# Second layer's input projections moved behind the whole first layer, with turned keys held on chip

## The chip, the core and the metric

The kernel runs on one core of one Trainium2 chip. The core has five engines with a queue each: PE (TensorE, matrix multiplies and their weight loads), DVE (VectorE), ACT (ScalarE), POOL (GpSimd) and SP (SyncE, which here issues nearly all DMA transfers). An engine works through its queue in order; an instruction that waits for a semaphore holds up all that stand behind it. The metric is the device time of one execution in microseconds (us), the median of several runs.

## What is computed

A decoder trunk of two layers over 2048 tokens of width 1024, all in float32. Layer 1 is an mLSTM mixer, layer 2 a dilated sliding-window attention; each is followed by a gated side term (`ple_add`). Keys and values of layer 2 come from the residual stream behind layer 1. Cut to layer 2, which the change is about:

```python
def shared_kv(h, norm_g, w_kv, knorm_g, cos, sin):          # 4 heads of 128
    k, v = jnp.split(rms_norm(h, norm_g) @ w_kv, 2, axis=-1)
    return apply_rope(rms_norm(k, knorm_g), cos, sin), v

def dilated_layer(h, k, v, norm_g, w_in, qnorm_g, w_out, cos, sin):
    q, z = jnp.split(rms_norm(h, norm_g) @ w_in, [1536], axis=-1)
    q = apply_rope(rms_norm(q, qnorm_g), cos, sin)          # 3 groups of 4 heads
    for g, (window, dilation) in enumerate(((128, 1), (512, 4), (2048, 16))):
        # query t sees t, t-r, t-2r, ..., t-window (r = dilation)
        o_g, l_g = dilated_window_attention(q[:, :, g], k, v, window, dilation)
    o = sum over g of softmax(l)[g] * o_g                   # l: log denominators
    return (o * silu(z)) @ w_out

h = h + mlstm_layer(h); h = ple_add(h)                      # layer 1
h = h + dilated_layer(h, *shared_kv(h)); h = ple_add(h)     # layer 2
```

The attention works on blocks of 128 queries: tokens of one residue modulo the dilation, against the 128 keys of the same block and, from the second block on, the 128 keys of the block before. Dilation 1 has 16 blocks, dilation 4 has 4 residues with 4 blocks each, dilation 16 has 16 residues with one block each.

## The kernel before

**Tiles.** The tokens are worked on in `NG` = 4 groups of `T` = 512 (`NT` = 4 tiles of 128 tokens). Activations X are kept as 8 pieces of 128 features by 512 tokens, each split into a high and a low fp32r part (`xh`, `xl`; `split`, L99 to L107). Weights are streamed from memory for each group: a raw piece (`wraw`, `raw_piece`, 5 buffers), its two parts (`wh`, `wl`, 5 buffers each), then three matmuls for each of four outputs (high by high, low by high, high by low).

**Projections.** `project` (L153) runs over the 8 pieces; one piece, 12 matmuls of 512 columns, is called a *step*. With `feat` set the outputs are features by tokens (L167), otherwise tokens by features (L169). Behind each step it calls a hook, if there is one for that step, and `pump`, which advances the list `side` by one turn. In this way work of other kinds stands between the steps on every engine's queue.

**Order.** For each group: `a_in` (projections and mLSTM of layer 1), `a_out` (output projection and `ple`, which writes h to `h2d` and splits h into X for layer 2), then `b_in`: keys, values, queries of dilation 16 (`queries(2)`), of dilation 4 and of dilation 1, and the gate z, six projections of 8 steps. Keys and queries go through `normrope` (norm and rotation, on DVE, ACT and POOL) and, like the values, to memory: `kd`, `vd`, `qd`.

**Attention.** A block is the generator `attend`, with five stages: load keys and queries (`kr`, `qr`); turn them by four transposes each on PE (`turned`, L664) and copy the result to `kT` (ACT) and `qT` (DVE); scores (L695) and softmax (L701 to L707); transposes of the probabilities (L715); product with the values (L726). A block whose predecessor isn't at hand also loads and turns the keys of the block before (`kp`). `staged` starts a block each turn and moves all started ones by a stage. The first list (14 blocks of dilation 4 and 1) runs beside the last group's `b_in`; at `late`, behind `queries(2)`, a second list is added with the remaining two, all of dilation 16, the last blocks of dilation 4, the four combinations `held_back` and the blocks of group 1 of dilation 1.

**Combination and end.** Dilation 4 and 16 leave their results in memory (`o1d`, `o2d`, with maxima and sums in 8 more columns). `combine` loads both (`oo`, 2 buffers) and `zt` (1 buffer), forms the weights and the sum y (L760 to L778, DVE and ACT) and multiplies by z (L780, POOL). y is turned (`transposed`, L182) and goes into the output projection and the second `ple`, again by groups, with the remaining blocks of dilation 1 between the steps.

The order on each queue is made by a scheduler from the order of the code and priorities (`PRE` for weights, `EVAC` for what empties a bank); buffers of one name are handed out in turn, and a tile waits until the one that had its buffer is read.

## Time and profile before

| | us |
|---|---|
| median of three runs | 2348.1 (2347.1 to 2356.36) |
| the profiled execution, whole | 2347.66 |
| its span, first to last instruction | 2345.8 |
| its mean granted TensorE clock | 0.997 |

The table's last three rows are of the one execution that the profile shows. The chain of work in order of time and the timelines place the parts of the program in the span: layer 1 and the `b_in` of the first three groups, and the last group's layer 1 but for its end, up to 1544 us; the last group's output projection and `ple`; its `b_in` with attention beside it from 1646.7 to 1932.3 us; a stretch of attention blocks and combinations without projections up to 1962.1 us; then the output projections of layer 2 to the end. In the 40 slices of the page these are slices 28 to 34.

PE's rows print a duration that runs on into the next instruction, since matmuls are pipelined. The distance between the starts of neighbouring rows is what an instruction takes from the queue.

### The profile page before, as it was taken

The numbers are of one execution on the slowest core, as the hardware profiler recorded it, in microseconds if no ns is written. First come the engines' busy times: TensorE is split into PE (matmuls) and PEld (weight loads), VectorE is DVE, ScalarE is ACT, GpSimd is POOL, SyncE is SP. The second block draws the span as 40 slices with busy tenths as digits, with TensorE's granted clock in tenths as the row PEclk, the third lists the DMA queues.
The fourth block names the chain that finished last, engine by engine and source line by source line (L and its number), as shares of the span: only waits on it lengthen the run. The fifth ranks groups of instructions, "written<-read, shape, count | busy, mean of one in ns | idle before, by whom it ended". The sixth has DMA issues, their size and how long they took to land.

```text
span 2345.8 us, 35374 instructions
## 1 busy us (share of the span) xinstructions
PE 2313.6 (99%) x11760; PEld 1977.5 (84%) x11760; DVE 1543.6 (66%) x3405; ACT 1128.3 (48%) x2731; POOL 593.0 (25%) x719
## 2 busy tenths in 40 slices
PE   9999999999999999999999999999999998999999
PEld 7889888888888888889888888888898887888887
DVE  6846665776566667747575675566755668786866
ACT  5434454543344545434444543344664666453643
POOL 5011235601211644011225601212202121220301
PEclk9999999999999999999999999999999999999999
DMA  5433344533244455333344543253674777465453
GB/s 184 125 91 115 99 149 162 183 116 121 61 123 125 146 164 165 117 91 111 103 130 142 174 125 120 64 171 117 203 221 134 231 237 228 135 198 164 145 160 98
DMA packets 190246, 337.14 MB, mean 144 GB/s; under 512 B 21552, under 2 KB 38256, under 8 KB 190064
## 3 DMA queue, kind: packets, MB, share of 16 engines
q1 hardware_dynamic: 189920, 334.86, 46.1%
q8 instruction: 93, 1.52, 0.3%
q14 instruction: 89, 0.73, 0.1%
q10 hardware_dynamic: 144, 0.02, 0.0%
HBM read 284.27 MB, written 50.53 MB: 143 GB/s over the span
## 4 chain that ended last, share of the span: by engine, by line
PE 85%; DVE 6%; DMA 4%; POOL 2%; ACT 2%; issue 1%; SPq 0%; ACTq 0%; DVEq 0%; POOLq 0%
PE bank L169 41%; PE bank L167 32%; PE bank L726 2%; PE bank L695 2%; PE bank L664 1%; DVE wl L104 1%; PE bank L525 1%; PE bank L526 1%; PE bank L528 1%; PE bank L715 1%; PE bank L182 1%; DMA oo<-o2d 1%; PE bank L512 1%; DMA o2d<-ot 1%; DVE xl L106 1%
## 5 line engine op out<-in xcount | busy, mean ns | idle before, releaser
L169 PE MATMUL bank<-wh,xh 128*128 128x512 f32 (+1 forms) x1664 | 642.5, 386 | 2.8 <-ACT wh L102 2.8
L169 PE MATMUL bank<-wl,xh 128*128 128x512 f32 (+1 forms) x1664 | 622.0, 374 | 0.8 <-DVE wl L104 0.8
L169 PE MATMUL bank<-wh,xl 128*128 128x512 f32 (+1 forms) x1664 | 622.6, 374 | 0.0
L102 ACT ACTIVATE wh<-wraw 128x512 fp32r<-128x512 f32 (+1 forms) x544 | 326.7, 603 | 549.5 <-PE bank L167 302.8
L104 DVE TENSOR_TENSOR wl<-wraw,wh 128x512 fp32r<-128x512 f32 (+1 forms) x512 | 353.9, 695 | 318.7 <-ACT wh L102 317.3
L167 PE MATMUL bank<-xh,wh 128*128 128x512 f32 x1272 | 501.9, 395 | 0.4 <-ACT xh L102 0.4
L167 PE MATMUL bank<-xh,wl 128*128 128x512 f32 x1272 | 496.0, 390 | 0.0
L167 PE MATMUL bank<-xl,wh 128*128 128x512 f32 x1272 | 495.9, 390 | 0.0
L169 PEld LDWEIGHTS bank<-wh,xh 128*128 128x128 f32 x1664 | 313.9, 189 | 51.0 <-ACT wh L102 3.1
L169 PEld LDWEIGHTS bank<-wh,xl 128*128 128x128 f32 x1664 | 313.4, 188 | 50.3
L169 PEld LDWEIGHTS bank<-wl,xh 128*128 128x128 f32 x1664 | 314.2, 189 | 49.3 <-DVE wl L104 1.2
L206 POOL TENSOR_TENSOR acc<-acc,sq 128x512 f32<-128x512 f32 x105 | 162.1, 1545 | 546.7 <-ACT sq L205 543.8
L167 PEld LDWEIGHTS bank<-xl,wh 128*128 128x128 f32 x1272 | 239.1, 188 | 50.5
L167 PEld LDWEIGHTS bank<-xh,wh 128*128 128x128 f32 x1272 | 239.4, 188 | 48.3 <-ACT xh L102 0.6
L167 PEld LDWEIGHTS bank<-xh,wl 128*128 128x128 f32 x1272 | 239.6, 188 | 47.8
L106 DVE SCALAR_TENSOR_TENSOR wl<-wraw,gam,wh 128x512 fp32r<-128x512 f32 x192 | 159.8, 833 | 154.1 <-ACT wh L102 151.5
L102 ACT ACTIVATE wh<-wraw,gam 128x512 fp32r<-128x512 f32 x192 | 138.0, 721 | 195.2 <-PE bank L169 134.8
L707 ACT ACTIVATE pr<-pr,nm 128x256 f32<-128x256 f32 (+1 forms) x192 | 86.6, 453 | 43.5 <-DVE nm L704 43.3
L601 POOL TENSOR_SCALAR ssb<-ssb,r 128x4 f32<-128x4 f32 x64 | 27.3, 426 | 254.1 <-ACT jk L194 233.0
L695 PE MATMUL bank<-kT,qT 128*128 128x128 f32 x600 | 78.5, 278 | 7.0 <-DVE pT L719 2.9
L695 PEld LDWEIGHTS bank<-kT,qT 128*128 128x128 f32 x600 | 72.8, 192 | 10.5 <-DVE pT L719 4.5
L726 PEld LDWEIGHTS bank<-vt,pT 128*128 128x128 f32 x600 | 75.3, 194 | 3.9
(413 smaller groups left out, 2957.4 us busy)
## 6 DMA issues: line engine op xcount, KB each, us to landing
wraw<-in_w_pg SPq DMA_DIRECT2D x128, 256.0 KB, 2.8
wraw<-in_w_in_b SPq DMA_DIRECT2D x128, 256.0 KB, 2.8
wraw<-in_w_z SPq DMA_DIRECT2D x96, 172.0 KB, 2.3
wraw<-in_w_v SPq DMA_DIRECT2D x64, 256.0 KB, 2.6
wraw<-in_w_o SPq DMA_DIRECT2D x64, 256.0 KB, 2.7
wraw<-in_w_out_a SPq DMA_DIRECT2D x64, 256.0 KB, 2.6
wraw<-in_w_kv SPq DMA_DIRECT2D x64, 256.0 KB, 2.7
kr<-kd SPq DMA_DIRECT2D x53, 256.0 KB, 4.2
```

The source lines that it names most:

```text
L102: nc.scalar.mul(dst_h, src, scale)
L104: nc.vector.tensor_tensor(dst_l, src, dst_h.bitcast(F32), op=ALU.subtract)
L106: nc.vector.scalar_tensor_tensor(dst_l, src, scale, dst_h.bitcast(F32), op0=ALU.mult, op1=ALU.subtract)
L167: nc.tensor.matmul(acc[i], w[:, cs], x, start=first, stop=last)
L169: nc.tensor.matmul(acc[i][:, :n], x[:, cs], w, start=first, stop=last)
L182: nc.tensor.transpose(tp[:, t * P:(t + 1) * P], tiles[t][:, k * P:(k + 1) * P], ident)
L206: eng.tensor_tensor(acc, acc, sq, op=ALU.add)
L512: nc.tensor.matmul(sp[:, h * P:(h + 1) * P], qk[:, NH + h, ts_], qk[:, h, ts_], start=True, stop=True)
L601: nc.gpsimd.tensor_scalar(ss, ss, r2[:, t:t + 1], EPS, op0=ALU.mult, op1=ALU.add)
L695: nc.tensor.matmul(sp[:, hh * n + j * P:hh * n + (j + 1) * P], qT[:, hs], kvs[j]["k"][:, hs], start=True, stop=True)
L707: nc.scalar.activation(pr[:, hh, :n], pr[:, hh, :n], AF.Exp, bias=nm[:, h:h + 1], accum_out=md[:, 4 + h:5 + h])
L726: nc.tensor.matmul(op[:, hs], pTs[h // 2][:, c0 + j * P:c0 + (j + 1) * P], kvs[j]["v"][:, hs], start=j == 0, stop=j == nk - 1)
```

## The change

- The loop over the groups runs all of layer 1 first; `b_in` follows for all four groups, as a phase of its own. `a_out` no longer splits h into X; `b_in` loads X from `h2d` (8 pieces for each group). The token norms for `b_in` (`rstb`) are made by a hook behind step `BH` = 3 of the following projection.
- `b_in` begins with `queries(2)`, then keys, values, the queries of dilation 4 and 1, and z.
- Keys aren't written to memory. `turn_key` transposes each tile of 128 tokens once, by hooks behind steps 3 to 6 of the value projection, into `kT`, which holds all keys (128 by 4 heads by 2048 tokens). `attend` reads the keys of a block out of `kT` with a step of 1, 4 or 16 columns.
- Attention blocks begin as soon as their group's projections are done: 8 blocks beside `b_in(1)`, 4 beside `b_in(2)`, 4 beside `b_in(3)`, the rest from two steps (`VP`) behind the values of the last group.
- Buffers: `wraw` 5 to 4, `pj` 8 to 7, `oo` 2 to 1; `kr` (2) and the 4 small `kT` are gone; `xraw` lives in another pool.

```diff
-        raw = wp.tile([P, n], F32, name="wraw", tag="wraw", bufs=5)
+        raw = wp.tile([P, n], F32, name="wraw", tag="wraw", bufs=4)
...
-        return sm.tile([P, n], F32, name="pj", tag="pj", bufs=8)
+        return sm.tile([P, n], F32, name="pj", tag="pj", bufs=7)
...
         def done(k, hk):
-            X2.append(new_x())
-            split(*X2[k], hk, 1.0)
             squares(sq2, k, hk)
             nc.sync.dma_start(h2d[g, k], hk)
 
         ple(0, g, h, X, sq, done)
-        return X2, sq2
+        return {BH: lambda: rstb.append(token_rstd(sq2, "rstb"))}
...
-    def b_in(g, X, sq, late=lambda: None):
+    def b_in(g, late=lambda: None, hooks={}):
+        X = []
+        for k in range(KD):
+            with tc.high_priority(offset=PRE):
+                raw = raw_piece(h2d[g, k], T)
+                X.append(new_x())
+                split(*X[k], raw, 1.0)
...
+        def keys():
+            acc = project(I["w_kv"][0], 512, 8, X, False, gam[:, G_KV])
+            obs = []
+            with tc.high_priority(offset=EVAC):
+                for t in range(NT):
+                    obs.append(normrope(acc[t], t, 0, 1.0, None, tabk[t]))
+            return {KT + t: lambda t=t: turn_key(g * NT + t, obs[t]) for t in range(NT)}
...
-        queries(2)
+        queries(2, hooks)
+        values(keys())
         late()
...
-    for g in range(NG - 1):
-        b_in(g, *a_out(g, *a_in(g)))
-    X, sq = a_out(NG - 1, *a_in(NG - 1))
+    late = {}
+    for g in range(NG):
+        late = a_out(g, *a_in(g, late))
     pa.close()
...
+    kT = bp.tile([P, NH, SEQ], F32, name="kT", tag="kT", bufs=1)
+
+    def turn_key(n, ob):
+        tp = bank()
+        for h in range(NH):
+            nc.tensor.transpose(tp[:, h * P:(h + 1) * P], ob[:, h * P:(h + 1) * P], ident)
+        nc.scalar.copy(kT[:, :, n * P:(n + 1) * P], tp.rearrange("p (h s) -> p h s", h=NH))
+
+    def key(h, r, res, b):
+        return kT[:, h, b * P * r:(b + 1) * P * r].rearrange("p (i r) -> p r i", r=r)[:, res]
...
-        kr = load(kd, r, res, b, "kr", 2)
         qr = load(qd, r, res, b, "qr", 2, grp * 512)
-        if prev == "load":
-            kp = load(kd, r, res, b - 1, "kr", 2)
         yield
-        kv["k"] = turned(kr, "kT", 4, nc.scalar.copy)
         qT = turned(qr, "qT", 2, nc.vector.tensor_copy)
         if prev == "load":
-            prev = {"k": turned(kp, "kT", 4, nc.scalar.copy), "v": load(vd, r, res, b - 1, "vt", 5)}
-        kv["v"] = load(vd, r, res, b, "vt", 5)
+            prev = load(vd, r, res, b - 1, "vt", 5)
+        vs = ([prev] if prev is not None else []) + [load(vd, r, res, b, "vt", 5)]
...
-                    nc.tensor.matmul(sp[:, hh * n + j * P:hh * n + (j + 1) * P], qT[:, hs], kvs[j]["k"][:, hs],
-                                     start=True, stop=True)
+                    nc.tensor.matmul(sp[:, hh * n + j * P:hh * n + (j + 1) * P], qT[:, hs],
+                                     key(h0 + hh, r, res, b + 1 - nk + j), start=True, stop=True)
...
-            oo = bp.tile([P, 2, 520], F32, name="oo", tag="oo", bufs=2)
+            oo = bp.tile([P, 2, 520], F32, name="oo", tag="oo", bufs=1)
...
-    first = group1(range(3), {}) + group0(0)
-    side.append(staged(first[:-NL]))
-    def tailed():
-        return group2() + group1((3,), {}) + last + group0(1)
-
-    b_in(NG - 1, X, sq, lambda: side.append(staged(first[-NL:] + tailed())))
+    def wait(n):
+        side.append(iter(range(n)))
+
+    b_in(0, hooks=late)
+    side.append(staged(group1((0,)) + group0(0)))
+    b_in(1)
+    side.append(staged(group1((1,))))
+    b_in(2)
+    side.append(staged(group1((2,))))
+
+    def rest():
+        drain()
+        wait(VP)
+        side.append(staged(group2() + group1((3,)) + last + group0(1)))
+
+    b_in(NG - 1, rest)
```

(`group0`, `group1` and `group2` list the blocks of dilation 1, 4 and 16.)

What this makes of the queues is shown at three places. The first is PE inside one step of attention beside `b_in`. The columns are the line, the operation, what it writes and reads, its shape and the count; `vt` are values, `pr` and `pT` probabilities, and line numbers differ between the two kernels. Before:

```order
L726 MATMUL bank<-vt,pT 128x128 x8
L715 MATMUL bank<-ident,pr 128x128 x8
L695 MATMUL bank<-kT,qT 128x128 x4
L664 MATMUL bank<-ident,kr 128x128 x4
L664 MATMUL bank<-ident,qr 128x128 x4
L169 MATMUL bank<-wh,xh 128x512
```

And the changed kernel, a step of the same kind:

```order
L757 MATMUL bank<-vt,pT 128x128 x8
L746 MATMUL bank<-ident,pr 128x128 x8
L726 MATMUL bank<-kT,qT 128x128 x8
L699 MATMUL bank<-ident,qr 128x128 x4
L171 MATMUL bank<-wh,xh 128x512
```

The set of four key transposes is gone from the step. (Counts are of the program; a 128 by 128 f32 matmul is two instructions on PE, a transpose one.)

The second place is PE in the stretch before the first output projection. Before, from the last product with the values that stands close behind another to the transposes of y:

```order
L726 MATMUL bank<-vt,pT 128x128 x8
L664 MATMUL bank<-ident,kr 128x128 x4
L664 MATMUL bank<-ident,qr 128x128 x4
L664 MATMUL bank<-ident,kr 128x128 x4
L695 MATMUL bank<-kT,qT 128x128 x8
L664 MATMUL bank<-ident,kr 128x128 x4
L664 MATMUL bank<-ident,qr 128x128 x4
L715 MATMUL bank<-ident,pr 128x128 x6
L695 MATMUL bank<-kT,qT 128x128 x2
L715 MATMUL bank<-ident,pr 128x128 x2
L664 MATMUL bank<-ident,kr 128x128
L695 MATMUL bank<-kT,qT 128x128 x6
```

In the changed kernel:

```order
L757 MATMUL bank<-vt,pT 128x128 x8
L699 MATMUL bank<-ident,qr 128x128 x4
L726 MATMUL bank<-kT,qT 128x128 x8
L699 MATMUL bank<-ident,qr 128x128 x4
L746 MATMUL bank<-ident,pr 128x128 x6
L726 MATMUL bank<-kT,qT 128x128 x2
L746 MATMUL bank<-ident,pr 128x128 x2
L726 MATMUL bank<-kT,qT 128x128 x6
L699 MATMUL bank<-ident,qr 128x128 x4
L184 MATMUL bank<-ident,y 128x128 x16
```

The same blocks stand in the same order, without four key sets (the last of them split over two rows before, of which the second is below the piece).

The third place is SP's queue in the same stretch: the loads for the combinations. Before, from the first `oo` load on:

```order
L751 DMA oo<-o2d 128x520
L658 DMA kr<-kd 128x512
L751 DMA oo<-o2d 128x520
L658 DMA qr<-qd 128x512
L111 DMA wraw<-in_pT 128x512
L658 DMA vt<-vd 128x512
L736 DMA o1d<-ot 128x520
```

In the changed kernel:

```order
L782 DMA oo<-o2d 128x520
L113 DMA wraw<-in_w_out_b 128x512
L693 DMA vt<-vd 128x512
L767 DMA o1d<-ot 128x520
L693 DMA vt<-vd 128x512
L693 DMA qr<-qd 128x512
L781 DMA oo<-o1d 128x520
L669 DMA zd<-pj 128x512
L693 DMA vt<-vd 128x512
L767 DMA o1d<-ot 128x520
```

The second tile's `oo` load stood directly behind the first one's; now its first half stands behind the work of two more blocks, with stores of `o1d` and loads of `vt` behind it.

More of the change, by code (lines that the diff above doesn't have):

```diff
@@ L35 @@
 EX = 3
+BH = 3
+KT = 3
+VP = 2
 HO = {0: (6,), 1: (7, 2), 2: (3,), 3: (4,), 4: (5,)}
@@ L321, in norms, with both, a_in @@
         return rstd_hooks(st, sq, N1, N2, "rba")
-    def a_in(g):
+    def both(a, b):
+        out = {s: [f] for s, f in a.items()}
+        for s, f in b.items():
+            out.setdefault(s, []).append(f)
+        return {s: lambda fs=fs: [f() for f in fs] for s, fs in out.items()}
+    def a_in(g, late):
         X = []
@@ L338, in a_in @@
         if g:
-            st, hooks = ahead.pop(g), {}
+            st, hooks = ahead.pop(g), late
         else:
@@ L615, in b_in, with queries @@
         nc.vector.scalar_tensor_tensor(r2, rst, 1.0 / P, rst, op0=ALU.mult, op1=ALU.mult)
[L616 to L628 removed]
+        def queries(grp, hooks={}):
+            acc = project(I["w_in_b"][grp], 512, 8, X, False, gam[:, G_B], hooks=hooks)
             with tc.high_priority(offset=EVAC):
@@ L810, in staged, with group1 @@
             yield
-    def group1(blocks, kvs):
+    def group1(blocks):
         return [lambda res=res, b=b: attend(
-            1, 4, res, b, kvs.setdefault((res, b), {}),
-            None if b == 0 else kvs.get((res, b - 1)) or "load", spill(o1d, 4, res, b))
+            1, 4, res, b, [], None if b == 0 else "load", spill(o1d, 4, res, b))
             for res in range(4) for b in blocks]
     def group2():
-        return [lambda res=res: attend(2, 16, res, 0, {}, None, spill(o2d, 16, res, 0)) for res in range(16)]
+        return [lambda res=res: attend(2, 16, res, 0, [], None, spill(o2d, 16, res, 0)) for res in range(16)]
     near, ys, done0 = {}, {}, []
@@ L826, in group0 @@
         return [lambda t=t, n=g * NT + t: attend(
-            0, 1, 0, n, near.setdefault(n, {}), near.get(n - 1) if n != NT else "load",
+            0, 1, 0, n, near.setdefault(n, []), None if n == 0 else "load" if n == NT else near[n - 1][0],
             keep(ys[0][t], held[t]) if g == 0 else combine(n)[0],
```

48 lines of the change are left out of this document (23 added, 25 removed).

## The prediction

> **What bounds the kernel now.** I read the page first: the busy times, the forty slices, the chain that ended last.
>
> ```profile
> span 2345.8 us, 35374 instructions
> ...
> PE 2313.6 (99%) x11760; PEld 1977.5 (84%) x11760; DVE 1543.6 (66%) x3405; ACT 1128.3 (48%) x2731; POOL 593.0 (25%) x719
> ...
> PE   9999999999999999999999999999999998999999
> ...
> PE 85%; DVE 6%; DMA 4%; POOL 2%; ACT 2%; issue 1%; SPq 0%; ACTq 0%; DVEq 0%; POOLq 0%
> ```
>
> TensorE is busy in every slice but one, and the chain lies on it for 85%. A busy PE need not be a PE at its pace, so the next view is a window over the attention stretch (b_in of the last group with attention between its matmuls), and then the list of what PE waited for.
>
> ```profile
> 1646.67:1922.53 275.86, 267.06 (x1766) 239.98 (x1764) 167.12 (x562) 170.28 (x562) 53.71 (x69) 0.99 0.65 205
> ```
>
> ```profile
> PE bank L715 <- ACT pr L707: 4.1, 5, 2.0
> PE bank L664 <- DMA qr<-qd: 3.5, 1, 3.5
> ...
> PE bank L664 <- DMA kr<-kd: 2.5, 1, 2.5
> PE bank L695 <- ACT kT L666: 1.9, 1, 1.9
> ...
> PE bank L695 <- ACT xh L102: 1.7, 1, 1.7
> ```
>
> Where attention runs, PE has 267 of 276 us, DVE 167 and ACT 170. No other engine is near the bound, the granted clock is 0.99, and all waits that PE has there are single ones of 1 to 4 us. So an instruction taken from PE in this stretch is worth its pitch, that is the distance to the start of the next one (the printed durations overlap), and an instruction taken from ACT or a queue is worth nothing by itself.
>
> **Key transposes taken away.** Before, a block turns its own keys, and a second set for the block behind it: 53 sets of four (212 transposes). The timeline of PE shows one set inside a step, and another view a lone set between two 512-wide matmuls.
>
> ```profile
> L664 PE MATMUL bank<-ident,kr x212: 270/273/328, 1652.1 to 2186.1; 128*128 128x128 f32 x106
> ...
> L666 ACT COPY kT<-bank x53: 560/583/592, 1653.7 to 2186.5; 128x512 f32<-128x512 f32 x53
> ```
>
> ```profile
> 1662.60 1.95 PE L695 MATMUL bank<-kT,qT 128*128 128x128 f32 x16
> 1664.39 0.60 PE L664 MATMUL bank<-ident,kr 128*128 128x128 f32 x4
> 1664.83 0.60 PE L664 MATMUL bank<-ident,qr 128*128 128x128 f32 x4
> 1665.18 0.48 PE L169 MATMUL bank<-wh,xh 128*128 128x512 f32 x1
> 1665.50 0.39 PE L169 MATMUL bank<-wl,xh 128*128 128x512 f32 x1
> 1665.73 0.40 PE L169 MATMUL bank<-wh,xl 128*128 128x512 f32 x1
> ```
>
> ```profile
> 2254.10 0.60 PE L182 MATMUL bank<-ident,y 128*128 128x128 f32 x4
> 2254.45 0.48 PE L167 MATMUL bank<-xh,wh 128*128 128x512 f32 x1
> 2254.77 0.40 PE L167 MATMUL bank<-xh,wl 128*128 128x512 f32 x1
> ```
>
> From 1664.39 to 1664.83 a key set costs 0.44 us; the query set behind it stays. A lone set costs 0.35, and the 512-wide matmul behind it 0.32 in place of 0.23 (1665.50 to 1665.73): 0.44 again. 49 of the 53 sets stand in stretches where PE has no slack; four stand in the end stretch (the order of PE in the part on the change), which is priced below. So 49 x 0.44 = **21.6 us go**. The change adds 16 lone sets, one for each 128 tokens, between the steps of the value projection: 16 x 0.44 = **7.0 us come**. With them 37 copies of 0.58 us leave ACT, which has slack; if its cover went they would be worth something only in the end stretch.
>
> A set added waits for its keys: normrope of four tiles behind the key projection, with three steps of twelve 0.23 us matmuls (8 us) before the first set and one step more before each next. I take no wait; one late set would hold PE, and all in its queue, for one step at most.
>
> The token norms of b_in (`rstb`) are asked for behind the fourth step of the next group's first projection, where they stood behind the sixth of b_in's own: a wait moved forward, with all of PE's queue behind it. They need POOL's running sum.
>
> ```profile
> L206 POOL TENSOR_TENSOR acc<-acc,sq 128x512 f32<-128x512 f32 x105 | 162.1, 1545 | 546.7 <-ACT sq L205 543.8
> ```
>
> The last four sums take 4 x 1.5 = 6.2 us once h is out; four steps of PE take 48 x 0.23 = 11. I take nothing; the other end is a step or 2.7 us at each of four groups, and goes with the late boundaries below.
>
> **Queues.** On SP 53 loads of kr and 16 stores of kd go, 32 loads of h2d and 8 of vt come: 29 fewer. The query tables are made before the key tables, the same POOL instructions. One raw weight buffer and one pj buffer fewer: a raw piece is let go once it is split, and five split pairs stand between it and PE, so I put this at nothing; without that cover, it would cost what is said under the boundaries below.
>
> **The keys are now read with a stride.** Blocks of dilation 4 and 16 take every fourth or sixteenth key column out of the resident kT. These are 112 + 64 matmuls of the program, each two instructions on PE: 352 of the 600 of this row.
>
> ```profile
> L695 PE MATMUL bank<-kT,qT 128*128 128x128 f32 x600 | 78.5, 278 | 7.0 <-DVE pT L719 2.9 <-ACT kT L666 1.9 <-ACT xh L102 1.7
> ```
>
> ```profile
> 1675.17 0.95 PE L215 MATMUL bank<-ones,acc 128*128 128x1 f32 x8
> 1675.98 0.47 PE L726 MATMUL bank<-vt,pT 128*128 128x128 f32 x2
> ...
> 152.40 0.59 PE L525 MATMUL bank<-v,ml 128*128 128x257 f32 x2
> 152.83 0.60 PE L526 MATMUL bank<-cstate,ml 128*128 128x257 f32 x2
> ```
>
> No row of before has a strided moving operand. What can be read is how much room there is. A key matmul has a pitch of 1.79 / 16 = 0.112 us. With one moving column (1675.17 to 1675.98, eight of them) it is still 0.101, so a pitch of 0.1 is there without any moving data. With 257 columns of plain f32 it is 0.43 / 2 = 0.215, 0.84 ns a column; an fp32r matmul takes 0.23 / 512 = 0.45 ns a column. So f32 columns already enter at about half the pace at which the same memory feeds fp32r. A stride that halves the pace of fp32r is hidden: nothing. A stride that halves the pace of f32 makes 128 columns as long as 256, and the nearest row has 0.215: (0.215 - 0.112) x 352 = 36 us. A gain is excluded, since the same data are read. I take **nothing**, because the fp32r rows show that the reading side has twice the pace needed, and keep 0 to 36 for the range.
>
> [...]
>
> **Starts of attention.** Before, attention starts twice within b_in, and PE waits at both: 1.7 us for a key copy that stands behind ACT's other work, and 3.5 us for the last queries' way through memory. Both reasons go (keys resident; dilation 16's queries are now projected first, two projections earlier): -5.2. In their place there are four starts, since each group from the second on begins its own list and the last has two. A start has few blocks in flight to stand between one block's scores and its transposes. One such start later in the program:
>
> ```profile
> 2081.37 0.33 PE L715 MATMUL bank<-ident,pr 128*128 128x128 f32 x1 [1.63 <-ACT pr L707]
> ```
>
> That wait is 1.63, the mean of its kind 4.1 / 5 = 0.8. I take 1.3: 4 x 1.3 = **+5.2, which cancels** the -5.2. Ends: 0, and four of 3.5, or 14. The lists before the last are short (8, 4 and 4 blocks for 48, 48 and 16 steps), so `drain` finds nothing left. The last list has 28 entries and begins two steps late (`VP`), where it had 30: as many are left over for the end stretch, 28 - 22 and 30 - 24.
>
> **The end stretch.** Between the last input projection and the first output projection four tiles are combined (L760 to L780). The rows are from the timelines of SP, DVE, POOL and PE.
>
> ```profile
> 1920.58 0.32 SPq L751 DMA_DIRECT2D oo<-o2d  x1
> ...
> 1924.73 0.16 DVE L760 TENSOR_TENSOR mm<-oo 128x4 f32<-128x4 f32 x1 [3.29 <-DMA oo<-o2d]
> ...
> 1930.71 1.14 DVE L778 SCALAR_TENSOR_TENSOR y<-oo,ee,y 128x128 f32<-128x128 f32 x4
> ...
> 1952.73 0.16 DVE L760 TENSOR_TENSOR mm<-oo 128x4 f32<-128x4 f32 x1 [0.67 <-DMA oo<-o2d]
> ...
> 1957.45 2.19 DVE L778 SCALAR_TENSOR_TENSOR y<-oo,ee,y 128x128 f32<-128x128 f32 x8
> ...
> 1959.71 1.26 POOL L780 TENSOR_TENSOR y<-y,zt 128x512 f32<-128x512 f32 x1 [7.00 <-DVE y L778]
> ...
> 1961.03 0.66 PE L182 MATMUL bank<-ident,y 128*128 128x128 f32 x4 [1.23 <-POOL y L780]
> ```
>
> A load takes 4.15 us (1920.58 to 1924.73), a combination 7.1 (to 1931.85) or 6.9 (1952.73 to 1959.64), and the last transposes of y wait for the fourth. With one oo buffer in place of two, a load starts only when the combination before it has read its last column: 1920.58 + 4 x (4.15 + 7.0) = 1965.2, and 1.3 for POOL: PE goes on at 1966.5 in place of 1961.0, **+5.5**. The waiting load stands on SP's queue, ahead of the vt loads and o1d stores behind it. Four key copies leave ACT and DVE is not interleaved with a second combination, so I take **+4**. The four key sets (1.8) and PE's waits for kr and kT (2.5 + 1.9) lie in the same stretch and bring nothing while y comes last; if the loads should hide after all, they are the other end: -6.2.
>
> **Boundaries.** X of b_in now comes from memory as 32 pieces in all; before, it was split out of h (as many splits).
>
> ```profile
> wraw<-in_xT SPq DMA_DIRECT2D x32, 256.0 KB, 3.0
> ```
>
> ```profile
> L104 DVE TENSOR_TENSOR xl<-h,xh 128x512 fp32r<-128x512 f32 x32 | 28.7, 898 | 2.9 <-ACT xh L102 2.6
> ```
>
> ```profile
> L102 ACT ACTIVATE xh<-h 128x512 fp32r<-128x512 f32 x32 | 20.0, 624 | 26.4 <-DVE h L298 26.4
> ```
>
> The layer-1 groups read X from memory in this way now, and no wait of PE stands at their starts. The work that hides it is the projection before, which frees X piece by piece. Cover gone, one piece is 3.0 + 0.6 + 0.9 = 4.5 us, at the seven boundaries that have a new neighbour (three of layer 1, four of b_in) 31.5. I take 0.
>
> **Sum.** -21.6 + 7.0 + 0 - 5.2 + 5.2 + 4 = -10.6 us. The profiled execution took 2347.66, 0.4 below the median of 2348.1 of the runs shown; from the median that is **2337 us**. Own range: both low ends (-6.2 and no start waits) give 2348 - 14.6 - 6.2 - 5.2 = 2322, both high ones (+5.5, 14) 2348 - 14.6 + 5.5 + 8.8 = 2348.
>
> **Rivals.**
> - *Strided keys are dear* (slower). Place: the key matmuls of dilations 4 and 16, all in PE-bound steps. Price up to 36 us: 2373. It turns the sign from 10.6 / 352 = 30 ns more for each, a pitch of 0.142. For it: no strided row exists to the contrary. Against it: the column paces above. 0.18.
> - *Better*: loads of oo hide partly (-3 in place of +4) and starts cost half: 2337 - 7 - 2.6 = 2327. For it: ACT and SP have less to do. Against it: the single buffer. 0.12.
> - *The sets don't come off the path*: a step's length is set by ACT or DVE once the transposes are gone, and the 14.6 come back: 2352. Against it: 267 of 276 us. 0.08.
> - *Boundaries are late*: X's pieces at half of the seven: 2337 + 16 = 2353. Against it: the like boundaries of before are free. 0.08.
>
> **The numbers.** The forecast has 0.54. A measurement of this kernel tells apart about 0.5%, 11.7 us: 2336.4 to 2359.8 counts as the same. The forecast's own range straddles the lower bound, a little under half below it: 0.26 faster, 0.28 same. Better adds 0.12 to faster; the sets, most of late boundaries and a mild stride add 0.15 to same; the rest, 0.19, is slower. So faster 0.38, same 0.43, slower 0.19. Range 2323 to 2366: it leaves out the dear end of the stride and little else.
>
> **What would show it.** Key sets: 64 transposes in the value projections, each lone set about 0.44 us between its neighbours; otherwise the third rival. Stride: the pitch of sixteen key matmuls in a dilation-4 block against that of a dilation-1 block, 0.112 both; 0.14 or more would make the prediction wrong by itself. Starts: PE's waits at the first pr transposes of four lists, 1.3 each. End stretch: the oo loads one behind another, each only after the L778 rows of the tile before, and PE's wait for POOL's y grown by some 4 us. Boundaries: no wait of PE for wraw or xh where b_in begins.

## The result, and the profile after

| | before | after |
|---|---|---|
| median of the runs | 2349.35 us (2347.1 to 2356.36) | 2424.79 us (2421.98 to 2427.54) |
| profiled execution, its span | 2347.66, 2345.8 | 2423.78, 2421.6 |
| granted clock of PE | 0.997 | 0.987 |

The ratio is 1.0316, 95% interval 1.029 to 1.0341: slower by 75 us, where 10.6 us less was forecast, and above the range. The page of the changed kernel, span and busy times (each engine with its share and number of instructions):

```profile
span 2421.6 us, 34918 instructions
...
PE 2359.4 (97%) x11612; PEld 2001.9 (83%) x11612; DVE 1545.7 (64%) x3405; ACT 1119.9 (46%) x2694; POOL 602.2 (25%) x719
```

PE runs 148 instructions fewer than before (the 212 transposes of `kr` and 64 of `turn_key`) and yet is busy for 46 us more. So part of the loss is inside PE's own work, and the rest in waits. The group of the key matmuls, with the mean of one, has the first part:

```profile
L726 PE MATMUL bank<-kT,qT 128*128 128x128 f32 x600 | 117.9, 352 | 5.3 <-DVE qT L701 5.3
```

The same 600 had 78.5 us and a mean of 278 ns before. The timeline of PE shows which: sixteen matmuls of a block of dilation 4, eight of dilation 16, eight of dilation 1, each with the row that follows it.

```profile
1768.88 3.79 PE L726 MATMUL bank<-kT,qT 128*128 128x128 f32 x16
1772.50 0.62 PE L699 MATMUL bank<-ident,qr 128*128 128x128 f32 x4
...
1905.55 1.90 PE L726 MATMUL bank<-kT,qT 128*128 128x128 f32 x8
1907.28 0.62 PE L699 MATMUL bank<-ident,qr 128*128 128x128 f32 x4
...
1455.28 1.14 PE L726 MATMUL bank<-kT,qT 128*128 128x128 f32 x8
1456.17 0.48 PE L171 MATMUL bank<-wh,xh 128*128 128x512 f32 x1
```

From start to start: 3.62 / 16 = 0.226 us with a step of 4, 1.73 / 8 = 0.216 with a step of 16, 0.111 with neighbours. The second part is in the list of PE's waits (total, times, longest):

```profile
PE bank L171 <- ACT wh L104: 12.4, 4, 4.3
PE bank L184 <- POOL y L811: 11.2, 2, 6.9
PE bank L240 <- DVE dg L231: 10.0, 5, 4.0
PE bank L746 <- ACT pr L738: 5.5, 6, 1.8
PE bank L726 <- DVE qT L701: 5.3, 4, 2.3
PE bank L217 <- POOL acc L208: 4.2, 4, 1.3
```

Before, `wh` had one wait of 2.8 near the program's beginning, `y` 1.2, `dg` 0.7, `acc` 0.2. Three of the waits for `wh` stand where `b_in(1)`, `b_in(2)` and `b_in(3)` begin: PE has done the last projection of the group before and has no first weights for the next. SP's timeline ahead of the first of them (1397.0 to 1400.8), and POOL's rows that it waits for:

```profile
1387.47 1.35 SPq L113 DMA_DIRECT2D wraw<-h2d  x3
1393.70 0.32 SPq L624 DMA_DIRECT2D qd<-pj  x1
1394.07 0.42 SPq L582 DMA_DIRECT2D cst<-in_cs  x1
1394.60 1.34 SPq L113 DMA_DIRECT2D wraw<-h2d  x3
1396.03 0.38 SPq L113 DMA_DIRECT2D wraw<-in_w_in_b  x1
```

```profile
1388.57 0.37 POOL L589 TENSOR_SCALAR tab<-tab 128x64 f32<-128x64 f32 x1
...
1392.31 1.36 POOL L622 TENSOR_TENSOR pj<-pj,rq 128x512 f32<-128x512 f32 x1
```

Between 1388.8 and 1393.7 SP issues nothing: its next instruction is a store of `qd`, which waits for POOL's last operation on that tile (ended 1393.67), and POOL works off rope tables and normrope in turn. Behind the store wait the last three of the eight pieces of X of the next group, and behind those its first weights. The piece issued at 1396.03 is split into `wh` at 1400.03, and PE stands for 3.8 us.

The end stretch went as the prediction's working had it, only further: SP's loads of `oo` come one tile at a time, each behind the combination before it (its last L809 row ended at 2003.56 and 2014.95).

```profile
2003.59 0.32 SPq L781 DMA_DIRECT2D oo<-o1d  x1
...
2014.98 0.32 SPq L781 DMA_DIRECT2D oo<-o1d  x1
...
2018.25 0.16 DVE L791 TENSOR_TENSOR mm<-oo 128x4 f32<-128x4 f32 x1 [3.30 <-DMA oo<-o2d]
...
2024.35 1.11 PE L184 MATMUL bank<-ident,y 128*128 128x128 f32 x4 [6.89 <-POOL y L811]
```

### The profile page after: what moved, and what is told of

It reads as the page before. It is cut to its first block, busy times and chain, and to the rows that moved or that the text cites. A ratio compares the mean times of both kernels' runs of the same rounds, so it can differ in the third digit from the quotient of the medians.

```text
span 2421.6 us, 34918 instructions
## 1 busy us (share of the span) xinstructions
PE 2359.4 (97%) x11612; PEld 2001.9 (83%) x11612; DVE 1545.7 (64%) x3405; ACT 1119.9 (46%) x2694; POOL 602.2 (25%) x719
## 5 line engine op out<-in xcount | busy, mean ns | idle before, releaser
L171 PE MATMUL bank<-wh,xh 128*128 128x512 f32 (+1 forms) x1664 | 648.7, 390 | 12.4 <-ACT wh L104 12.4
L106 DVE TENSOR_TENSOR wl<-wraw,wh 128x512 fp32r<-128x512 f32 (+1 forms) x512 | 365.8, 718 | 301.3 <-ACT wh L104 299.4
L169 PE MATMUL bank<-xh,wh 128*128 128x512 f32 x1272 | 505.2, 398 | 2.2 <-ACT wh L104 1.7
L169 PE MATMUL bank<-xh,wl 128*128 128x512 f32 x1272 | 499.0, 392 | 0.0
L169 PE MATMUL bank<-xl,wh 128*128 128x512 f32 x1272 | 499.0, 392 | 0.0
L169 PEld LDWEIGHTS bank<-xl,wh 128*128 128x128 f32 x1272 | 240.8, 189 | 51.7 <-DVE xl L106 0.2
L169 PEld LDWEIGHTS bank<-xh,wh 128*128 128x128 f32 x1272 | 241.1, 190 | 51.3 <-ACT wh L104 2.1
L169 PEld LDWEIGHTS bank<-xh,wl 128*128 128x128 f32 x1272 | 241.4, 190 | 48.5
L108 DVE SCALAR_TENSOR_TENSOR wl<-wraw,gam,wh 128x512 fp32r<-128x512 f32 x192 | 153.6, 801 | 186.9 <-ACT wh L104 181.1
L726 PE MATMUL bank<-kT,qT 128*128 128x128 f32 x600 | 117.9, 352 | 5.3 <-DVE qT L701 5.3
L618 POOL TENSOR_SCALAR ssb<-ssb,r 128x4 f32<-128x4 f32 x64 | 27.6, 431 | 357.2 <-ACT jk L196 352.8
L726 PEld LDWEIGHTS bank<-kT,qT 128*128 128x128 f32 x600 | 99.9, 202 | 12.1 <-ACT wh L104 5.4
L732 DVE CUSTOM_DVE_ANT_0 pr<-bank,masks 128x256 f32<-128x256 f32 (+1 forms) x192 | 64.8, 361 | 45.8 <-PE bank L726 45.5
```

The source lines that it names most:

```text
L106: nc.vector.tensor_tensor(dst_l, src, dst_h.bitcast(F32), op=ALU.subtract)
L108: nc.vector.scalar_tensor_tensor(dst_l, src, scale, dst_h.bitcast(F32), op0=ALU.mult, op1=ALU.subtract)
L169: nc.tensor.matmul(acc[i], w[:, cs], x, start=first, stop=last)
L171: nc.tensor.matmul(acc[i][:, :n], x[:, cs], w, start=first, stop=last)
L618: nc.gpsimd.tensor_scalar(ss, ss, r2[:, t:t + 1], EPS, op0=ALU.mult, op1=ALU.add)
L726: nc.tensor.matmul(sp[:, hh * n + j * P:hh * n + (j + 1) * P], qT[:, hs], key(h0 + hh, r, res, b + 1 - nk + j), start=True, stop=True)
```

## The experiments

Theories after the result: the stride (A), buffers given up to make room for the resident keys (B: `oo`, `wraw`, `pj`), the queue at the boundaries (C: tables and stores ahead of the loads), the half clock behind idle time (D: 0.50 in after behind a wait of 3.8 us, shown with e7), and the new order itself (E). All times are in the table at the end of this part.

**e1, e2: the stride.** Edits of `key` in the changed kernel; both read the wrong keys, with the same instructions. e1, neighbouring columns:

```diff
-        return kT[:, h, b * P * r:(b + 1) * P * r].rearrange("p (i r) -> p r i", r=r)[:, res]
+        c = b * P * r + res * P
+        return kT[:, h, c:c + P]
```

and e2, small steps:

```diff
-        return kT[:, h, b * P * r:(b + 1) * P * r].rearrange("p (i r) -> p r i", r=r)[:, res]
+        c, step = b * P * r + res, {1: 1, 4: 2, 16: 3}[r]
+        return kT[:, h, c:c + step * (P - 1) + 1:step]
```

> Each strided read of the keys (dilations 4 and 16) takes 128 neighbouring columns of kT instead; the scores of those blocks are of the wrong keys, and the same number of instructions runs. If the stride is what made the score matmuls slow: all L726 instructions come at the pitch of the dilation-1 blocks, 0.112 us instead of 0.22, and the time falls by about 35 us, from 2425 to 2385-2393. If something else slows them (writes of kT or the rest of attention beside them): pitch stays near 0.22 in those blocks and the time stays within 5 us of 2425.

> Dilation 4 reads its 128 keys at a step of 2 columns (8 bytes), dilation 16 at a step of 3 (12 bytes); the scores of those blocks are of the wrong keys, the same number of instructions runs. If the cost goes by 16-byte lines touched: 64 lines at step 2 stay at the pitch of 0.112 us, 96 lines at step 3 come to about 0.168, so the 224 instructions of dilation 4 give back 23 us and the 128 of dilation 16 about 7: 2425 falls to 2392-2400. If any step doubles the read: pitch 0.22 in both, no change (within 5 us of 2425). If only bytes between neighbours count (cost grows with the step): 0.15-0.19 in both.

Measured: e1 2396.35, 28.4 less than after and 3 above its range; e2 2400.56, 24.2 less and 0.6 above its own. The groups of the key matmuls in e1 and in e2, and in e2's timeline a block with step 2 and one with step 3:

```profile
L727 PE MATMUL bank<-kT,qT 128*128 128x128 f32 x600 | 81.6, 283 | 9.2 <-DVE qT L702 8.6 <-ACT ot L766 0.6
```

```profile
L727 PE MATMUL bank<-kT,qT 128*128 128x128 f32 x600 | 87.4, 294 | 6.9 <-DVE qT L702 6.9
...
1763.53 2.01 PE L727 MATMUL bank<-kT,qT 128*128 128x128 f32 x16
1765.38 0.60 PE L700 MATMUL bank<-ident,qr 128*128 128x128 f32 x4
...
1842.67 1.55 PE L727 MATMUL bank<-kT,qT 128*128 128x128 f32 x8
1844.05 0.61 PE L700 MATMUL bank<-ident,qr 128*128 128x128 f32 x4
```

Step 2 (64 lines) runs at 1.85 / 16 = 0.116 us, step 3 (96) at 1.38 / 8 = 0.173: as the count of 16-byte lines had it (0.112 and 0.168), and as neither of the other two readings had. With 128 lines it is 0.226 (step 4) and 0.216 (step 16). So the stride is shown as the cause of the slow key matmuls, and from 96 lines on the pitch goes with the count of lines of four f32, at 1.69 to 1.80 ns each. The line itself is a unit of counting that fits these pitches; no trace shows it. Of the 36 us that e1 takes from the group, 28 arrive: PE's waits for `qT` and `pr` grow from 10.8 to 16.3.

**e5: the same without leaving anything out.** The keys of 512 tokens lie in the order (token mod 16, token div 16); masks and rows of V follow.

```diff
+            to = kT[:, h, w * T:(w + 1) * T].rearrange("p (r i) -> p r i", r=16)
+            nc.scalar.copy(to[:, :, q * 8:(q + 1) * 8], tp[:, h * P:(h + 1) * P].rearrange("p (i r) -> p r i", r=16))
...
+        if r == 4:
+            return kT[:, h, b * T:(b + 1) * T].rearrange("p (m s i) -> p s m i", m=4, s=4)[:, res]
...
+            src = vd[b * P:(b + 1) * P, :].rearrange("(i a) c -> a i c", a=16)
```

> kT holds each 512 tokens in the order (token mod 16, token div 16), so that every dilation reads runs of 8 or 32 neighbouring columns; masks and V rows of dilations 1 and 4 follow the same order, and the result is the whole computation. If 16-byte lines are all that made the score matmuls slow: L726's pitch is 0.112 us everywhere and the time is that of e1 (2396), within 6 us. If the 64 smaller copies into kT on ACT or the row order of the V loads cost: pitch 0.112 all the same, but waits for kT, vt or pr grow, and the time is 2403 to 2420.

Measured: 2422.78, as good as nothing gained, although the key matmuls are as fast as in e1:

```profile
L752 PE MATMUL bank<-kT,qT 128*128 128x128 f32 x600 | 81.9, 283 | 11.5 <-DVE qT L727 6.3 <-ACT ot L791 5.1
```

```profile
PE bank L171 <- ACT wh L104: 17.0, 5, 5.6
...
PE bank L752 <- ACT ot L791: 5.1, 4, 2.1
PE bank L783 <- DVE pT L776: 3.4, 1, 3.4
```

Against e1, PE's idle time (span less busy time) is 13.1 us longer: the waits for `wh` (+4.4), `ot` (+4.5; one buffer, filled again only behind its stores: in after the engines of its copies sit idle for 15.0 us until these have landed) and `pT` (+3.4) are most of it. Its busy time is 13.4 us longer for the same number of instructions (2337.2 and 2323.8), at a granted clock of 0.982 against 0.986. So the 26 us between e1 and e5 are placed, but which part of the layout brings the waits wasn't taken apart. The second expectation was right in kind and too small.

**e3, a13, a14, a16, e9: the buffers.** e3, a13 and a14, in this order, each give one buffer back to the changed kernel (room comes from small tiles of layer 1, moved to its own pool):

```diff
-            oo = bp.tile([P, 2, 520], F32, name="oo", tag="oo", bufs=1)
+            oo = bp.tile([P, 2, 520], F32, name="oo", tag="oo", bufs=2)
...
-        return sm.tile([P, n], F32, name="pj", tag="pj", bufs=7)
+        return sm.tile([P, n], F32, name="pj", tag="pj", bufs=8)
...
-        raw = wp.tile([P, n], F32, name="wraw", tag="wraw", bufs=4)
+        raw = wp.tile([P, n], F32, name="wraw", tag="wraw", bufs=5)
```

a16 takes one from the kernel before, and e9 takes `pj` 8 to 7 and `oo` 2 to 1 as well:

```diff
-        raw = wp.tile([P, n], F32, name="wraw", tag="wraw", bufs=5)
+        raw = wp.tile([P, n], F32, name="wraw", tag="wraw", bufs=4)
```

> Two buffers for the loads of the combination again (oo), with the room taken from small tiles that only the first layer uses. If the single buffer makes the late end of attention: PE's wait for y (L811) falls from 11.2 to under 3 us, its wait for dg (L231) in the output phase from 10.0 to under 2, the half clock behind them goes too, and the time falls by 18 to 30 us, to 2395-2407. If POOL's and DVE's backlog is late by itself: the waits keep over half their length and the time falls by under 8 us.

> The kernel before with the buffers of the changed one: wraw 4 for 5, pj 7 for 8, oo 1 for 2; its order and key path stay. If the buffers alone make the late end of attention: waits for y and dg of 8 to 20 us appear here too and the time is 2360 to 2372. If it takes the new order as well (stores, tables and loads of X meeting in one queue): within 6 us of 2350, with no wait for wh above 1 us.

> The changed kernel with eight buffers of pj again (room from small tiles that only the first layer uses). One projection's normrope takes two pj for each of four tiles. If the seventh-buffer limit is what makes SP's queue late at the boundaries: the waits for wh of 12.4 us shrink under 4 and the time is 2404 to 2414. If wraw is the cause: within 5 us of 2425 and the waits stay.

> The changed kernel with five buffers of wraw again. If the pieces of X and of weights, which pass through wraw in one order, stand one too few at the boundaries: the waits for wh of 12.4 us shrink under 4 and the time is 2400 to 2414, and the waits for dg in the output phase shrink too if those come from late weights. If pj is the cause: within 5 us of 2425.

> The kernel before with four buffers of wraw, nothing else. If wraw carries what e3 leaves of e9's 38 us: waits for wh of over 8 us and 2362 to 2376. If pj carries it: within 4 us of 2350.

Measured: `oo` in e3 gives 15.1 us, 3 under its expectation, `wraw` in a14 15.8, `pj` in a13 nothing (2429.8; its interval overlaps that of after; since a13 moves the same small tiles, their move gives nothing by itself either). In the old order a single `wraw` buffer costs 18.3 (a16), and all three edits 37.6 in e9, more than was expected of it. PE's waits in e3 (`dg` is halved, `y` has left the head of the list), a14 and a16:

```profile
PE bank L171 <- ACT wh L104: 12.7, 4, 4.1
...
PE bank L240 <- DVE dg L231: 4.5, 3, 3.1
...
PE bank L184 <- POOL y L811: 0.2, 1, 0.2
```

```profile
PE bank L184 <- POOL y L811: 11.2, 2, 7.0
PE bank L240 <- DVE dg L231: 9.6, 4, 4.4
...
PE bank L171 <- ACT wh L104: 5.2, 3, 3.5
```

```profile
PE bank L167 <- ACT wh L102: 12.5, 4, 5.2
PE bank L715 <- ACT pr L707: 3.9, 5, 1.8
```

Each buffer answers to its own wait: `oo` to `y` and `dg`, `wraw` to `wh`. a16 is the plainest: 2.8 us of waiting for `wh` become 13.0 (the 12.5 shown and 0.5 at L169) in a kernel in which nothing else has changed; three of the four waits shown stand where the next `a_in` begins, whose X comes through `wraw` too.

**e4, e7: the queue and the clock.** e4 has the rope tables on DVE, five lines like this one:

```diff
-            nc.gpsimd.tensor_tensor(tab[:, 0, a], q[:, a], c, op=ALU.mult)
+            nc.vector.tensor_tensor(tab[:, 0, a], q[:, a], c, op=ALU.mult)
```

e7 puts 18 matmuls of 128x512 into the last projection of `b_in`:

```diff
+        def fill():
+            wb = bank()
+            for _ in range(18):
+                nc.tensor.matmul(wb, X[0][0][:, 0:P], X[0][0], start=True, stop=True)
...
+        acc = project(I["w_in_b"][3], 512, 8, X, False, gam[:, G_B], hooks={5: fill} if g + 1 < NG else {})
```

> The five operations of each rope table run on DVE instead of POOL; nothing else changes. If POOL's tables hold SP's queue (the loads of cst and the stores of normrope behind them, and the pieces of X and weights behind those): PE's waits for wh at the three starts of b_in (4.4, 4.3 and 4.4 us) fall to under 1.5 each and the stretches at half clock behind them go, so that the time falls by 12 to 24 us, to 2401-2413. If the stores alone hold the queue, or the loads of X come too late by themselves: the waits keep over half and the time stays within 6 us of 2425.

> The changed kernel with 18 matmuls of 128x512 (0.227 us each, 4.1 us, into a bank that nobody reads) put where PE waits for wh in the last projection of b_in(0), b_in(1) and b_in(2). If the idle time is what brings the half clock: the waits there shrink to under 0.8 us, the matmuls behind them come at 0.23 us instead of 0.43 at once, and the time falls by 6 to 12 us although work is added. If the clock goes by something else: the pitch stays 0.43 there, and the time is the same or up to 3 us longer.

Measured: e4 2411.19, 13.6 us less, and no wait for `wh` is left at the boundaries; 7.6 us of it come back as waits for `qT` (12.9 in place of 5.3), three of them of 3.7 to 4.0 us where attention begins. DVE now has the tables there; that these hold the copy of `qT` is read from the place and not shown by a run.

e7 is 2441.43, 16.6 us longer, and doesn't decide what it was made for. Its expectation had the place wrong: the wait stands behind the last projection, and the 18 matmuls two steps ahead of it, in busy time. The first wait shrinks from 3.8 and 0.6 us to these, in PE's timeline of e7:

```profile
1408.23 0.51 PE L171 MATMUL bank<-wh,xh 128*128 128x512 f32 x1 [0.69 <-ACT wh L104]
1409.73 0.50 PE L171 MATMUL bank<-wl,xh 128*128 128x512 f32 x1 [0.99 <-DVE wl L108]
...
1411.04 0.63 PE L171 MATMUL bank<-wh,xl 128*128 128x512 f32 x1
1411.47 0.63 PE L171 MATMUL bank<-wh,xh 128*128 128x512 f32 x1
```

In all, the waits for `wh` fall from 12.4 to 1.9 us; but those for `qT`, `qr`, `acc` and `wl` grow, so that PE's idle time is 64.5 us against 62.2 and the added 12 us of work are not paid for. The pitch of 0.43 us (1411.04 to 1411.47) is still there behind it, for seven matmuls where after has nine. What these slow stretches cost by themselves, no run here tells apart. (6.4 of e7's 17 us stand in the first layer, whose instructions on PE are the same in both; so far can two profiled runs differ.) The clock behind the same wait in after, by windows (length; busy time of PE, PEld, DVE, ACT, POOL; granted clock, DMA share, GB/s):

```profile
1396.80:1400.80 4.00, 0.23 (x2) 0.00 (x1) 2.14 (x3) 2.61 (x4) 3.83 (x7) 0.87 0.55 185
1400.80:1405.80 5.00, 4.37 (x9) 3.10 (x10) 2.32 (x4) 1.45 (x2) 0.16 (x1) 0.50 0.76 261
1405.80:1411.00 5.20, 5.20 (x24) 4.25 (x23) 3.08 (x5) 4.05 (x7) 3.88 (x10) 0.92 0.58 181
```

**e8, e10, e11: key path and order.** e8 is the changed kernel with keys stored, loaded and turned by each block again (61 sets); e10 the same with `wraw` 5, `pj` 8, `oo` 2; e11 the old order with resident keys in e5's layout. The key path of e8 and e10:

```diff
+        krs = [load(kd, r, res, b, "kr", 2)]
...
+        ks = [turned(k, "kT", 6, nc.scalar.copy) for k in krs]
```

The part of e11 that turns the twelve tiles of the groups before (three at a time):

```diff
+    def early(n0):
+        ks = [pj() for n in range(3)]
...
+            turn_key(n0 + j, k)
+    side.append(staged([lambda n0=n0: early(n0) for n0 in range(0, 12, 3)] + first[:-NL]))
```

> The changed kernel with the key path of before (keys stored in memory, loaded and turned by each block; 61 sets of four transposes, for the 16 of turn_key): the reads are contiguous. If a set costs PE 0.44 us as lone instructions: 45 sets more are +20 us over e1's 2396, so 2411 to 2421. If the sets were hidden in waits anyway: within 5 us of 2396. If the loads of the keys are late in the queue as well: above 2425.

> The changed order (projections of the second layer as a phase, attention begun group by group) with the key path and all buffers of the kernel before: wraw 5, pj 8, oo 2; 61 sets of transposes. If the order costs by itself what e3, e4 and e8 leave over: waits for wh at the three boundaries stay near 4 us each, the wait for y is gone, and the time is 2395 to 2412, 2 to 2.6% above the kernel before with only 12 sets (5 us) more. If the buffers were the cause: under 2370.

> The order of the kernel before, with resident keys in the permuted layout: twelve tiles loaded and turned at the start of the last b_in, four turned as they come, no sets in the blocks (16 for 49); wraw 4, pj 7, oo 2; the whole computation. If the sets lie on the path: 33 x 0.44 = 14.5 us less, 2330 to 2341, faster than the kernel before. If the time goes into waits of attention as in e5 (ot, pr, vt): 2345 to 2362. If the late start of attention shows at the end: above 2362.

Measured: e8 2424.28, 27.9 over e1. The 45 further sets are 20 us by the price of 0.44, and the keys' way through memory brings waits of 7.8:

```profile
PE bank L689 <- DMA kr<-kd: 7.8, 2, 5.6
```

Both together are 27.6, but other waits are shorter than in e1 (`pr` 1.8 for 7.7), and PE's idle time is only 3.5 us longer. Its busy time is 25.0 us longer (2348.8 and 2323.8), 22.5 of it in the rows of the sets, 0.50 for each of the 45. So the sets do lie on PE's path, at somewhat over 0.44 here. And e8 equals after: turned once with a stride costs what turning each time costs. e10 is 2388.58, 35.7 less than e8, by the three buffers alone, about what e9 lost (37.6). Its expectation had the waits for `wh` stay with the order; they went with the buffers (one of 2.3 near the beginning is left). What e10 still loses to the kernel before, 37 us, is mostly one wait, which the changed kernel hasn't: stored keys are asked for at once where attention starts (three of the four, 23.2 us).

```profile
PE bank L689 <- DMA kr<-kd: 25.1, 4, 9.8
PE bank L721 <- DVE qT L691: 4.3, 3, 2.7
```

e11 is 2381.18, slower than the kernel before and above 2362, where its third expectation put a late end. 18.3 of it is the price of `wraw` 4 (a16). What is left, 2381.2 - 18.3 + 14.5 - 2350.6 = 27, is as much as the layout cost in e5, but it is a remainder and holds `pj` 7 too. Of that end PE's waits show something (`dg` 6.2, `y` 1.7), of attention's chain more (`pr` 9.5, `ot` 5.0, `pT` 4.1).

**e6, e12, a15, a17, a18: mended.** e6 joins e5, e3 and e4, makes the tables of the keys only when needed and puts off each start by two steps; e12 takes `ot` from the seven `pj`, moves the token norms two steps later and makes the tables of the queries one by one behind four steps of `queries(2)`; a15 adds `wraw` 5 and `pj` 8; a17 has `wraw` 6 and `pj` 7; a18 is the kernel before with `wraw` 6.

The first line is e6's, at three starts; the others are e12's.

```diff
+    wait(VP)
     side.append(staged(group1((1,))))
...
-BH = 3
+BH = 5
...
-        tabs = [rope_table(g, t, 1) for t in range(NT)]
+        tabs = []
...
-        queries(2, hooks)
+        late_tabs = {1 + t: lambda t=t: tabs.append(rope_table(g, t, 1)) for t in range(NT)}
+        queries(2, both(hooks, late_tabs))
...
-            ot = bp.tile([P, 520], F32, name="ot", tag="ot", bufs=1)
+            ot = pj(520)
```

> The permuted keys, two buffers of oo and the tables on DVE (the keys' tables only as the keys need them) together, and each start of attention put off by two steps. If the three prices add: -28, -15 and -14 from 2425, and the four waits for qT at the starts (5 to 13 us in all) shrink to under 3: 2352 to 2366, and no more than 0.7% above the kernel before. If they share the same idle time: 2370 to 2385. If freeing them lets the half-clock stretches go altogether: under 2350, faster than the kernel before.

> As e6, and the staged output ot takes the seven buffers of pj, and the sum over tokens (token_rstd) of the next group stands two steps later. If ot's one buffer held attention (7.7 us waited for it in e6) and the hook 5 us: 2368 to 2376. If the time is bound by the pace of one block's chain: within 4 us of 2383, the waits for pr and pT growing as those for ot go.

> e12 with wraw 5 and pj 8, so that it has all buffers of the kernel before; masks and a few constants stand elsewhere to make room. If e12's waits for wh, wl and jk (5.0, 2.8 and 6.5 us) come from those two: 2340 to 2350, at or just under the kernel before. If the pace of the attention's chain holds: within 4 us of 2359. Under 2340 only if the half clock goes too.

> a15 with six buffers of wraw and seven of pj (a13 showed pj without effect in the changed kernel). If the supply through wraw still binds with five: the waits for wl and dg go and the time is 2336 to 2347, faster than the kernel before. If five is enough: 2350 to 2357.

> The kernel before with six buffers of wraw (xraw moved to a pool of the first layer). If the supply still binds: 2336 to 2346. If five is enough there, as its waits for wh of 2.8 us in all let expect: within 4 us of 2350.

Measured: 2382.96, 2359.11, 2353.36, 2348.01 and 2350.96. e6 lies in its second range (2370 to 2385: the edits share the same idle time) and 17 us above the first. But sharing isn't needed to explain that: e5's layout gives nothing by itself, and the sum of e3, e4 and e5 as measured is 2394, 11 above e6. e12 gave 24 us where 7 to 15 were expected, with an edit (the tables of the queries) that its expectation doesn't name; no run parts the three. a15 and a17 each came out between their two expectations. a17 is the first that isn't above the kernel before, and a18 shows that a sixth buffer brings nothing to the old order. What PE still waits for in a17:

```profile
PE bank L776 <- ACT pr L768: 6.8, 6, 2.5
PE bank L729 <- ACT jk L193: 6.5, 3, 2.2
PE bank L787 <- DVE pT L780: 3.8, 2, 3.1
PE bank L237 <- DVE dg L228: 3.8, 3, 3.1
```

No wait for `wh` or `y` is left. `dg` belongs to the output phase; a wait of 2.7 us for `pj` is the copy of `ot` under its new name; the others shown are attention's own chain.

| kernel | median, us | ratio to before, 95% interval |
|---|---|---|
| after | 2424.79 | 1.0316 (1.029 to 1.0341) |
| e1, keys side by side | 2396.35 | 1.0194 (1.0172 to 1.0217) |
| e2, steps 2 and 3 | 2400.56 | 1.022 (1.0194 to 1.0246) |
| e3, `oo` 2 | 2409.72 | 1.0251 (1.0229 to 1.0273) |
| e4, tables on DVE | 2411.19 | 1.0259 (1.0231 to 1.0287) |
| e5, permuted keys | 2422.78 | 1.03 (1.0285 to 1.0315) |
| e6, e3 + e4 + e5 | 2382.96 | 1.0142 (1.0114 to 1.017) |
| e7, filled waits | 2441.43 | 1.0379 (1.0363 to 1.0394) |
| e8, keys turned again | 2424.28 | 1.0309 (1.0294 to 1.0325) |
| e9, before, fewer buffers | 2389.42 | 1.0158 (1.0141 to 1.0175) |
| e10, e8 with all buffers | 2388.58 | 1.0158 (1.0143 to 1.0173) |
| e11, old order, keys once | 2381.18 | 1.0126 (1.0109 to 1.0143) |
| e12, e6 mended further | 2359.11 | 1.0033 (1.002 to 1.0046) |
| a13, `pj` 8 | 2429.8 | 1.034 (1.0326 to 1.0354) |
| a14, `wraw` 5 | 2409.02 | 1.0249 (1.0235 to 1.0263) |
| a15, e12 with all buffers | 2353.36 | 1.0016 (1.0007 to 1.0025) |
| a16, before, `wraw` 4 | 2368.61 | 1.0085 (1.0069 to 1.01) |
| a17, a15 with `wraw` 6 | 2348.01 | 0.9989 (0.9979 to 0.9999) |
| a18, before, `wraw` 6 | 2350.96 | 0.9997 (0.9987 to 1.0007) |

## Why the prediction was wrong, step by step

- **The sets: right.** -21.6 + 7.0, at 0.44 each: from start to start the 53 sets of before take 23.2 us (0.44 each) and the 16 of after 5.7 (0.36, as a lone set was read). e8 against e1 has them on the path, with 25 us more of busy time for 45 sets. The gain is there; others eat it. The third rival falls.
- **The stride: the step that failed first.** It said "I take nothing, because the fp32r rows show that the reading side has twice the pace needed". That counts bytes. Counted in lines of 16 bytes, the fp32r matmul reads 512 columns, or 128 lines, in 0.227 us, and a strided key matmul 128 lines too, one for each column: at the pace of that row it takes about 0.22, and it does (0.216 to 0.226). The row was in the trace of before; the unit was wrong. (The row alone only said that a line takes no longer than that; that it takes no less either came with after and e2.) The rival of the strided keys, with a chance of 0.18, had place and price (36 us on PE, 28.4 in the time).
- **`wraw`: the second.** It said "five split pairs stand between it and PE, so I put this at nothing", and that failed: 15.8 us (a14), 18.3 in the old order (a16). The split pairs cover a piece of weights, but where a group begins, its eight pieces of X and its first weights go through the same ring, and the weights stand behind the X.
- **Boundaries: taken at 0, the same place.** "The layer-1 groups read X from memory in this way now, and no wait of PE stands at their starts" was true of the old order with five buffers and is false with four (a16's waits stand at just those starts). In the changed kernel the starts of layer 1 still have none; three of the seven boundaries have one, all of `b_in`, for `wh` and not for X, with 3.8, 4.3 and 3.8 us (4.4, 4.3 and 4.4 with the wait for `wl` behind it), close to the 4.5 of the bound. The rival of late boundaries, 16 us at 0.08, had this place. What holds the queue is the store of `qd` behind POOL's tables: e4 ends these waits too, so e4 and a14 are two prices of one wait and don't add.
- **The end stretch: mechanism right, size off.** +4 was taken (5.5 worked out), 15.1 measured. The loads did come one behind another, and PE's wait for `y` is 11.2. Left out: `dg` is late in the output phase too (10.0 us, 4.5 with two `oo`). That it comes through SP's and DVE's queues, which the late loads and combinations hold, is likely and not shown.
- **Starts of attention: about the size that was taken,** but not as told: three of the four starts have a wait, for `qT` and not `pr`, of 2.3, 1.4 and 0.6 us (the fourth wait of that line, 1.0, stands in the end stretch). 4.3 us stand against 4 x 1.3.
- **Token norms: taken at 0, 4.2 us of waits,** four for `acc` of up to 1.3 us. **`pj`: taken at 0, rightly** (a13).

The prices of the single steps, -14.6 for the sets, +28.4, +15.8, +15.1 and +4.2, make +48.9 (the starts nearly cancel the -5.2, as forecast). The other 26 of 75 us have no single edit to their name: the single edits were measured with all other faults in place, and where two faults share a stretch, mending one can leave the other's wait (in e4 7.6 us came back as waits for `qT`). That together they hold nearly all is shown by a15, which differs from after in these, in `ot`, the tables, the starts and the token norms, and stands 71 us below it.

The two profiled executions show the same 75 us in another division, by what PE does. Its idle time is 62.2 us against 32.2: +30. The strided reads are +36 (busy time of after less that of e1), the 37 sets that are gone -16. That leaves some 26 us by which the instructions common to both kernels run longer (that this is also the remainder above is chance, since the prices of the edits hold part of it). Nearly all of it is in the 7700 matmuls of 512 columns, which take 1775.8 us before and 1801.8 after, idle time left out; about 17 us are in those at half granted clock or next to it, 7 before and 81 after. (A clock of 0.5 stands for 17.5 us in 4 stretches before, for 65 in 11 after.) This term the prediction didn't have at all: here a wait costs PE its own length, and slow matmuls stand behind it (0.43 us in place of 0.23 behind the 3.8 us at 1400.80). Two profiled executions can differ by some microseconds in this, as e7's first layer did (6.4 us).

a17, with the sets gone and these waits mended, is 4 us faster than the kernel before (2348.01 and 2352.01), and not 14.6. Its profiled execution, 4 us longer than that of before, has 5.3 us more idle time on PE, and only 1.3 less busy time where 37 sets would be 16 less: here too the common instructions take 15 us longer. Its granted clock is 0.992 against 0.997, by estimate 12 us on 2350. So what the sets gave is taken by 5 us of waits and by longer matmuls, by this estimate in good part at a lower clock. No run separates the clock from the waits that it follows.

## What to carry to other kernels

When an operand is to be read with a stride, count the lines of 16 bytes that it touches, not only its bytes, and compare with the row of the fastest dense read, counted in the same lines: here 128 lines took 0.216 to 0.226 us strided and 0.227 dense. When a change needs memory, price each buffer that it gives up as an edit of its own, in the old kernel if need be: here each of two buffers out of three cost as much (15.8 and 15.1 us) as the whole feature could bring (14.6). And where loads of two kinds share a ring and a queue, look for the store or table that stands ahead of them, since its wait is theirs: here 4.9 us of SP (1388.8 to 1393.7) stood ahead of 3.8 us of PE.

## What the runs showed of the hardware that was not expected

- Counted in lines of 16 bytes, the moving operand of PE came in at 1.7 to 1.8 ns for each, dense fp32r (128 lines, 0.227 us) and strided f32 (96 lines 0.173, 128 lines 0.216 to 0.226) alike; with 64 lines (0.116) or 32 (0.111) the f32 matmul stayed near its own pitch of 0.112. Whether the dense fp32r matmul is held by its lines or only runs at the same pace isn't shown.
- Behind 3.8 us of idle time (1397.03 to 1400.80 in after) PE has a granted clock of 0.50 and a pitch of 0.43 us in place of 0.23 for some 5 us. In e7 less was enough: one matmul ran between 1407.5 and 1409.7, with waits of 0.69 and 0.99 us around it, and the pitch still fell to 0.43 a microsecond later. In after's trace ten of the eleven stretches at 0.50 begin between 2.2 us before and 2.7 us after the end of a wait of 1.3 to 4.3 us, and in that of before three of the four within 0.7 us of the end of one of 1.9 to 3.5 us (the last stretch of each is the program's end). But not every such wait has one: in after none stands behind the 2.2 us that end at 86.65, nor in before behind 1.9 and 2.5 us at 1948.88 and 1953.39. What length of wait brings it, the traces don't show.
